# Moving the weight tiles and the shared tiles of a two-block transformer kernel by 64 bytes in the SBUF partition

## The chip, the cores and the metric

One core of one Trainium2 chip runs the whole kernel. The metric is the device time of one execution in microseconds; the kernel before has a median of 3667.25 us over three runs (3667.17 to 3675.36).

## The reference

Two transformer blocks follow each other over a sequence of 512 tokens of 1024 channels, two layers each, in float32. The first block has adaptive modulation, a SwiGLU feed-forward (FFN) before and after a mixer of sparse attention and a gated MLP. The second has pooling in its first layer and attention over latent and context tokens in its second, each followed by a squared-ReLU MLP; the 256 context tokens go through the first layer only. Nearly all of the arithmetic is dense matrix products such as

```python
def _swiglu(x, w_in, w_out):
    a, b = jnp.split(x @ w_in, 2, axis=-1)
    return (jax.nn.silu(a) * b) @ w_out
...
def sq_relu_mlp(h, w_in, w_out):
    return jnp.square(jax.nn.relu(h @ w_in)) @ w_out
```

## The kernel before

Activations are held with channels on the partitions, in 8 chunks of 128, and 512 tokens along the partition. A product is made in three TensorE passes: each operand x is split into a high part (x rounded to `float32r`) and a low part (x minus the high part), and `mm3` (lines 113 to 116) adds high x high, high x low and low x high in one PSUM bank. `dense` (line 118) does that over the 8 chunks of the contraction, 24 matmuls of 128 x 128 weights and 512 (or, for context tokens, 256) columns.

`T.matmul(ps, w, x)` takes the weights as the stationary operand and the activations as the moving one. In the products that leave tokens on the partitions (`tok_proj`, lines 619 and 1431, and `values`) the activations are the stationary operand and 256 or 280 columns of weights move.

The weights come by DMA on SP's queue, 4 KB of each partition at a time, into `raw` (`wload`, line 91). `wsplit` (line 96) makes `whi` on ScalarE and `wlo` on VectorE, or on GpSimd where `cur["lo"]` says so. `raw`, `whi` and `wlo` have three buffers each, so a product's weights are made while the one before it runs. Products whose weights go at once are `Pre.issue` (line 283, matmuls on line 301) and `Pre.product` (line 328); they start on `h` times its gains before the norm is known.

The moving operands are these tiles:

- `n0` and `n1` (in the trace `n`), the normed input of a block, and `m` in the mixer's output product, 8 chunks each;
- `r`, 16 tiles of 512 columns (line 111) that hold hidden units, heads, or what `Pre` uses;
- `hid`, a few more tiles for hidden units. `HID_R` (line 468) says which of a part's 8 chunks lie in `hid` (0) and which in `r` (1). The FFN's hidden units go in parts of 8, 8 and 6 chunks; the last part lies in `hid` alone, but for the last FFN. The MLPs of the second block have two of eight chunks in `hid`, with `q` 0 and 4 (lines 1365 and 1583);
- `nc` and `hc`, for the context tokens: 256 columns, moved against the same `whi` and `wlo`. Their products are woven between those of the latent tokens (`weave`, line 1318).

The pools are laid out in the partition in the order in which they are opened, each tile rounded up to 32 bytes. `top` opens `const`, `resid`, `wraw`, `whi`, `wlo`, `r`, `norm`, `shp` and `small` first (lines 60 to 68); all pools of the stages come behind `small`. `const` starts at byte 16512, a multiple of 128, and has `par` (392 columns, 1568 bytes), `ident` (512) and `ones` (8, rounded to 32): 2112 bytes, 64 more than a multiple of 128. The pools from `resid` to `shp` take multiples of 128, so they all start at 64 past a multiple, and so does `small`, whose first tile is `pad` (line 71), 32 bytes that nothing reads. `small` ends so that the pools of the stages start at a multiple of 128. Before the change the tiles lie so:

| tiles | start, beyond a multiple of 128 bytes |
|---|---|
| `h`, `raw`, `whi`, `wlo`, `r`, `norm`, `shp` | 64 |
| `n`, `m`, `nc`, `hc`; `qT`, `kT`, `vl`, `pth`, `ptl` of the attentions | 0 |
| `hid` | 0; 64 in the last FFN |
| `adaw`, `junk`, `crow` of the modulation vectors | 0; 64 in the last FFN |
| temporaries of the FFN and MLP stages (2112 bytes each) | 0 and 64 by turns |
| `ident` | 32 |

Inside a tile every chunk of weights (512 bytes) and of activations (2048 or 1024 bytes) keeps the tile's place. Nothing in the kernel orders the work by place; the order of instructions is the order of the program on each engine, apart from the weaving of fillers (`run_steps`).

Of the kernel before, what the change touches and what calls it, by code (L numbers as in the profile page):

```python
# [9 lines left out]
F32 = mybir.dt.float32  # L10
# [29 lines left out]
PCOLS = {}  # L40
_n = 0
for _name, _w in (
    ("c", 8), ("c_2", 8), ("c_ctx_2", 8), ("norm_g", 48), ("final_g", 8), ("ada_b", 144),
    ("b_ada_2", 96), ("g_mix_pre_2", 16), ("g_mix_post_2", 16), ("g_mlp_pre_2", 16),
    ("g_mlp_post_2", 16), ("pool_scale_2", 8),
):
    PCOLS[_name] = _n
    _n += _w
# [3 lines left out]
def build(tc, d, stop=99):  # L52
    nc = tc.nc
    V, A, G, T, SY = nc.vector, nc.scalar, nc.gpsimd, nc.tensor, nc.sync
    top = ExitStack()

    def pool(st, name, bufs=1, **kw):
        return st.enter_context(tc.tile_pool(name=name, bufs=bufs, reuse_waits="tile", **kw))

    const = pool(top, "const")  # L60
# [7 lines left out]
    small = pool(top, "small", 2)  # L68
    aux = pool(top, "aux", 2, space=PSUM)

    G.memset(small.tile([128, 8], F32, name="pad", tag="pad", bufs=1), 0.0)

    par = const.tile([128, NPC], F32, name="par")
    SY.dma_start(par, d["par"])
    ident = const.tile([128, 128], F32, name="ident")
    ones = const.tile([128, 2], F32, name="ones")
    V.memset(ones, 1.0)
    h = resid.tile([128, DC, S], F32, name="h")

# [1640 lines left out]
```

## Time and profile before

| | |
|---|---|
| median of three runs | 3667.25 us (3667.17 to 3675.36) |
| the profiled execution's own time | 3675.36 us |
| its span, first to last instruction | 3673.6 us |
| instructions | 44524, of them 16932 matmuls |
| mean granted TensorE clock | 0.973 |
| DMA | 455.24 MB, 124 GB/s over the span |

PE stands for TensorE's matmuls, PEld for its weight loads, DVE for VectorE, ACT for ScalarE, POOL for GpSimd and SP for the engine whose queue issues the DMAs. A row `mm<-n,whi` is a matmul that writes the tile `mm` and reads `n` and `whi`; L114 is line 114. Matmuls overlap, so a row's mean duration is longer than the time from one matmul's start to the next one's. A clock of 1.00 is 2.4 GHz, 0.50 is 1.2 GHz.

### The profile page before, as it was taken

The page shows a single profiled execution, that of the slowest core. Times are in us where ns is not written, and L with a number is a line of the kernel's source. Part 1 is how long each engine was busy: PE and PEld are TensorE (multiplying, and loading weights), DVE is VectorE, ACT ScalarE, POOL GpSimd, SP SyncE. Part 2 cuts the span into 40 slices and gives each one's busy share as a digit, 9 for nine tenths or more (in the row PEclk, how much of TensorE's full clock was granted, in tenths as well). Part 3 has the DMA queues.
Part 4 walks back from the last instruction along what each step waited for, and adds up shares of the span by engine and source line. Part 5 has one row for each costly group of instructions (what it writes and reads, how often), then busy time and mean ns, then how long its engine had stood idle before and what let it go on. Part 6 is the DMA issues. An engine that isn't in the chain of part 4 may idle for free.

```text
span 3673.6 us, 44524 instructions
## 1 busy us (share of the span) xinstructions
PE 3491.0 (95%) x16932; PEld 2880.7 (78%) x16932; DVE 2301.8 (63%) x3656; ACT 1450.0 (39%) x2467; POOL 522.1 (14%) x493
## 2 busy tenths in 40 slices
PE   6999999999999999999999999989999978989998
PEld 5888886788878888887787877778888878767886
DVE  8863777458754995488647855665444587655434
ACT  4222465433223322366634223544333344634222
POOL 3000413030001200142004000340000052130000
PEclk8999989999999999999999999979999988999999
DMA  6862321237852573221134842314334331013332
GB/s 239 283 207 92 99 71 47 71 116 246 293 182 92 179 240 126 92 94 58 44 100 160 284 139 85 95 40 128 119 119 122 113 113 59 7 41 101 95 98 69
DMA packets 139254, 455.24 MB, mean 124 GB/s; under 512 B 16676, under 2 KB 19104, under 8 KB 138912
## 3 DMA queue, kind: packets, MB, share of 16 engines
q1 hardware_dynamic: 139040, 452.39, 38.1%
q8 instruction: 133, 2.18, 0.2%
q14 instruction: 81, 0.66, 0.1%
HBM read 450.23 MB, written 2.10 MB: 123 GB/s over the span
## 4 chain that ended last, share of the span: by engine, by line
PE 45%; DVE 6%; POOL 2%; ACT 2%; issue 1%; DMA 1%; DVEq 0%; SPq 0%; ACTq 0%; POOLq 0%
PE mm L114 12%; PE mm L116 12%; PE mm L115 12%; DVE ssum L150 1%; POOL shp L269 1%; DVE h L1077 1%; PE aux L862 0%; PE aux L1540 0%; PE mm L1443 0%; PE mm L1444 0%; PE mm L1445 0%; PE o L830 0%; POOL shp L274 0%; DVE wlo L100 0%; ACT whi L98 0%
## 5 line engine op out<-in xcount | busy, mean ns | idle before, releaser
L98 ACT ACTIVATE whi<-raw 128x1024 fp32r<-128x1024 f32 (+2 forms) x636 | 620.1, 977 | 1504.8 <-PE mm L115 1018.9
L100 DVE TENSOR_TENSOR wlo<-raw,whi 128x1024 fp32r<-128x1024 f32 (+3 forms) x584 | 677.9, 1162 | 513.1 <-ACT whi L98 507.9
L114 PE MATMUL mm<-n,whi 128*128 128x512 f32 x2096 | 831.8, 397 | 13.8 <-ACT nt L220 9.2
L116 PE MATMUL mm<-n,wlo 128*128 128x512 f32 x2096 | 826.0, 395 | 7.1 <-DVE wlo L100 7.0
L115 PE MATMUL mm<-n,whi 128*128 128x512 f32 x2096 | 823.5, 393 | 0.4 <-DVE n L224 0.2
L116 PEld LDWEIGHTS mm<-n,wlo 128*128 128x128 f32 x2096 | 396.0, 189 | 98.7 <-DVE wlo L100 10.4
L114 PEld LDWEIGHTS mm<-n,whi 128*128 128x128 f32 x2096 | 396.7, 189 | 97.7 <-issue 11.3
L115 PEld LDWEIGHTS mm<-n,whi 128*128 128x128 f32 x2096 | 396.4, 189 | 85.6 <-DVE n L224 0.9
L399 DVE SCALAR_TENSOR_TENSOR junk<-adaw,crow 128x1024 f32<-128x1024 f32 x288 | 353.4, 1227 | 78.9 <-DMA adaw<-adaT 58.8
L114 PE MATMUL mm<-r,whi 128*128 128x512 f32 x960 | 380.5, 396 | 6.5 <-ACT whi L98 5.9
L116 PE MATMUL mm<-r,wlo 128*128 128x512 f32 x960 | 379.1, 395 | 0.0
L115 PE MATMUL mm<-r,whi 128*128 128x512 f32 x960 | 376.1, 392 | 0.8 <-DVE r L108 0.8
L150 POOL TENSOR_TENSOR ssum<-ssum,sq 128x512 f32<-128x512 f32 x30 | 45.4, 1514 | 1293.7 <-ACT sq L149 1293.6
L114 PEld LDWEIGHTS mm<-r,whi 128*128 128x128 f32 x960 | 181.1, 189 | 45.8 <-ACT whi L98 6.4
L116 PEld LDWEIGHTS mm<-r,wlo 128*128 128x128 f32 x960 | 180.9, 188 | 42.2 <-DVE wlo L100 0.5
L115 PEld LDWEIGHTS mm<-r,whi 128*128 128x128 f32 x960 | 181.2, 189 | 41.7 <-DVE r L108 1.4
L100 POOL TENSOR_TENSOR wlo<-raw,whi 128x1024 fp32r<-128x1024 f32 (+1 forms) x52 | 108.9, 2102 | 637.1 <-ACT whi L98 630.4
L114 PE MATMUL mm<-hid,whi 128*128 128x512 f32 x448 | 176.8, 395 | 0.0
L116 PE MATMUL mm<-hid,wlo 128*128 128x512 f32 x448 | 175.6, 392 | 0.0
L115 PE MATMUL mm<-hid,whi 128*128 128x512 f32 x448 | 174.8, 390 | 0.0
L539 DVE SCALAR_TENSOR_TENSOR h<-mm,hg,h 128x512 f32<-128x512 f32 x96 | 71.8, 748 | 134.1 <-PE mm L116 134.1
L301 PE MATMUL mm<-r,whi 128*128 128x512 f32 x384 | 128.6, 410 | 18.4 <-ACT r L241 17.0
(472 smaller groups left out, 5807.0 us busy)
## 6 DMA issues: line engine op xcount, KB each, us to landing
adaw<-adaT SPq DMA_DIRECT2D x240, 512.0 KB, 4.9
raw<-ffn_in SPq DMA_DIRECT2D x170, 512.0 KB, 4.5
raw<-mlp_in SPq DMA_DIRECT2D x96, 512.0 KB, 3.8
raw<-ffn_out SPq DMA_DIRECT2D x64, 512.0 KB, 4.1
raw<-mlp_out SPq DMA_DIRECT2D x64, 512.0 KB, 3.7
raw<-mlp_out SPq DMA_DIRECT2D x64, 256.0 KB, 2.9
raw<-ffn_out SPq DMA_DIRECT2D x32, 384.0 KB, 3.1
raw<-mix_zb SPq DMA_DIRECT2D x16, 512.0 KB, 3.5
```

Source lines behind the costliest of these rows:

```text
L98: A.activation(hi[:, :F], raw, AF.Copy)
L100: (eng or cur["lo"]).tensor_tensor(lo[:, :F], raw, hi[:, :F], op=OP.subtract)
L114: T.matmul(ps, lh, rh, start=start, stop=False)
L115: T.matmul(ps, lh, rl, start=False, stop=False)
L116: T.matmul(ps, ll, rh, start=False, stop=stop)
L150: self.last = (eng or V).tensor_tensor(self.acc, self.acc, sq, op=OP.add)
L269: G.tensor_tensor(o.rearrange("p (k m) -> p k m", k=n), raw[:, k * 128:(k + n) * 128].rearrange("p (k m) -> p k m", k=n), self.sh[:, k:k + ...
L301: T.matmul(self.pss[n], w[:, sl], x, start=k + e == 0, stop=k == DC - 1 and e == 2)
L399: V.scalar_tensor_tensor(junk, w, 1.0, cs[v], op0=OP.mult, op1=OP.mult, accum_out=mods[v][:, j * 8 + m:j * 8 + m + 1])
L539: V.scalar_tensor_tensor(h[:, m], ps, hg[:, m:m + 1], h[:, m], op0=OP.mult, op1=OP.add)
L1077: V.tensor_tensor(x[:, k], t, x[:, k], op=OP.add)
```

## The change

`par` loses three groups of columns, 24 in all (96 bytes), that no line reads: `c`, `c_2` and `c_ctx_2` come by DMAs of their own (line 388). `const` gets a tile `pad0` of 32 bytes behind `ones`. Together `const` becomes 2048 bytes, and the pools from `resid` to `shp` start 64 bytes lower, at multiples of 128. `pad` in `small` grows by 64 bytes, so that everything behind it keeps its address. `ident` moves from 32 to 64 past a multiple of 128. No product, split or copy is changed, nor is the order of anything; one memset of GpSimd is added. In the table above the first row becomes 0, `ident` 64, and the rest stays.

```diff
 for _name, _w in (
-    ("c", 8), ("c_2", 8), ("c_ctx_2", 8), ("norm_g", 48), ("final_g", 8), ("ada_b", 144),
+    ("norm_g", 48), ("final_g", 8), ("ada_b", 144),
     ("b_ada_2", 96), ("g_mix_pre_2", 16), ("g_mix_post_2", 16), ("g_mlp_pre_2", 16),
     ("g_mlp_post_2", 16), ("pool_scale_2", 8),
 ):
...
-    G.memset(small.tile([128, 8], F32, name="pad", tag="pad", bufs=1), 0.0)
+    G.memset(small.tile([128, 24], F32, name="pad", tag="pad", bufs=1), 0.0)
 
     par = const.tile([128, NPC], F32, name="par")
     SY.dma_start(par, d["par"])
     ident = const.tile([128, 128], F32, name="ident")
     ones = const.tile([128, 2], F32, name="ones")
+
+    G.memset(const.tile([128, 8], F32, name="pad0"), 0.0)
     V.memset(ones, 1.0)
     h = resid.tile([128, DC, S], F32, name="h")
```

## Rows read from the trace of the kernel before

**Rows 1.** Busy times of the page: us, share of the span, instructions.
```profile
PE 3491.0 (95%) x16932; PEld 2880.7 (78%) x16932; DVE 2301.8 (63%) x3656; ACT 1450.0 (39%) x2467; POOL 522.1 (14%) x493
```

**Rows 2.** Busy time by stage: us, busy of each engine, PEclk, DMA share, GB/s.
```profile
92.00:410.00 318.00, 315.86 (x1373) 257.52 (x1371) 190.33 (x261) 93.43 (x116) 17.53 (x17) 0.99 0.54 181
776.50:819.00 42.50, 42.50 (x187) 34.75 (x186) 29.79 (x33) 18.68 (x26) 23.08 (x22) 1.00 0.34 107
1330.00:1418.00 88.00, 88.00 (x386) 72.19 (x385) 76.86 (x120) 25.26 (x32) 0.00 (x0) 1.00 0.65 209
3231.00:3273.00 42.00, 42.00 (x187) 34.75 (x186) 14.87 (x14) 16.40 (x26) 20.73 (x26) 1.00 0.26 80
```

**Rows 3.** Groups by line and form: count, busy us, mean ns, idle before.
```profile
L114 PE MATMUL mm<-n,whi 128*128 128x512 f32 x2096 | 831.8, 397 | 13.8 <-ACT nt L220 9.2 <-DVE rp L645 4.2 <-DVE px L377 0.3
...
L114 PE MATMUL mm<-r,whi 128*128 128x512 f32 x960 | 380.5, 396 | 6.5 <-ACT whi L98 5.9 <-ACT r L107 0.5
...
L114 PE MATMUL mm<-hid,whi 128*128 128x512 f32 x448 | 176.8, 395 | 0.0
...
L114 PE MATMUL mm<-nc,whi 128*128 128x256 f32 x272 | 79.5, 293 | 9.4 <-ACT nc L107 9.1 <-ACT whi L98 0.2
```

**Rows 4.** One tile's matmuls (n, m) in two stretches: ns min/median/max, first and last start.
```profile
L116 PE MATMUL mm<-n,wlo x128: 392/392/394, 1330.5 to 1417.7; 128*128 128x512 f32 x128
...
L116 PE MATMUL mm<-m,wlo x64: 387/394/397, 776.2 to 819.5; 128*128 128x512 f32 x64
```

**Rows 5.** The same view of r, attention's output product, 3229 to 3276 us.
```profile
L115 PE MATMUL mm<-r,whi x64: 389/389/393, 3230.6 to 3273.4; 128*128 128x512 f32 x64
L116 PE MATMUL mm<-r,wlo x64: 388/389/389, 3230.8 to 3273.7; 128*128 128x512 f32 x64
```

**Rows 6.** Timeline of PE in an FFN output product: start, duration.
```profile
161.14 0.40 PE L114 MATMUL mm<-hid,whi 128*128 128x512 f32 x1
...
162.53 0.40 PE L114 MATMUL mm<-r,whi 128*128 128x512 f32 x1
...
164.62 0.39 PE L114 MATMUL mm<-r,whi 128*128 128x512 f32 x1
...
166.66 0.40 PE L114 MATMUL mm<-hid,whi 128*128 128x512 f32 x1
```

**Rows 7.** Timeline of PE, matmuls of 256 columns in two stages.
```profile
2804.91 0.28 PE L114 MATMUL mm<-hc,whi 128*128 128x256 f32 x1
...
2805.97 0.39 PE L114 MATMUL mm<-hid,whi 128*128 128x512 f32 x1
...
3099.74 0.28 PE L1443 MATMUL mm<-whi,r 128*128 128x256 f32 x1
...
3100.82 0.28 PE L1443 MATMUL mm<-whi,r 128*128 128x256 f32 x1
```

**Rows 8.** Line 399 on VectorE, from 1330 to 1418 and from 2100 to 2188 us.
```profile
L399 DVE SCALAR_TENSOR_TENSOR junk<-adaw,crow x41: 1215/1224/1227, 1329.2 to 1401.3; 128x1024 f32<-128x1024 f32 x41
...
L399 DVE SCALAR_TENSOR_TENSOR junk<-adaw,crow x14: 1216/1226/1227, 2099.1 to 2131.0; 128x1024 f32<-128x1024 f32 x14
```

**Rows 9.** DMA issues (KB each, median us to landing), and the memset of pad.
```profile
raw<-ffn_in SPq DMA_DIRECT2D x12, 256.0 KB, 6.0
h<-xT SPq DMA_DIRECT2D x8, 256.0 KB, 6.3
...
L71 POOL MEMSET pad<- x1: 105/105/105, 0.7 to 0.7; 128x8 f32 x1
```

**Rows 10.** Timeline of PE, two runs in the second attention.
```profile
3140.79 0.39 PE L114 MATMUL o<-pth,vl 128*128 128x512 f32 x1
...
3141.47 0.60 PE L1540 MATMUL aux<-ident,p 128*128 128x128 f32 x4
...
3168.01 0.40 PE L114 MATMUL o<-pth,vl 128*128 128x512 f32 x1
...
3170.10 0.27 PE L202 MATMUL aux<-ident,rs 128*128 128x128 f32 x1
```

## The prediction

> **What bounds the kernel now.** I read the busy times first: PE is busy for 95% of the span [rows 1]. The table by stage says it more sharply: from 92 to 410 us PE is busy for 315.86 of 318.00 us, VectorE for 190.33 and ScalarE for 93.43 [rows 2]. PE sets the pace of this kernel, and what makes its matmuls longer or shorter is mostly on the path. So the question is a small one, asked many times: how far apart do two dense matmuls start? The groups by form give the counts [rows 3]: with 512 columns, three lines times 2096 on `n`, 960 on `r`, 448 on `hid`; with 256 columns, three times 272 on `nc`. By the loops of the context's second product there are three times 256 on `hc`.
>
> The reader should not look at the mean duration of a matmul (395 ns and the like): they overlap. The pitch is what counts, the time from one start to the next, and two streams of like products differ in it, though the granted clock is 1.00 in each, 2.4 GHz, and PE never rests [rows 2]. In a product on `n`, line 116 starts 128 times from 1330.5 to 1417.7 us: 87.2 us for 127 triples, 381 matmuls, 228.9 ns each; in the mixer's output product on `m`, 43.3 us for 189, 229.1 ns [rows 4]. In the attention's output product on `r`, line 115 gives 42.8 us for 189, 226.5 ns, and line 116 42.9, 227.0 ns: 226.7 between them [rows 5]. The weights are in the same `whi` and `wlo` in all of them, at 64 past a multiple of 128 bytes. The moving operand is not: `n` and `m` lie at a multiple of 128, `r` at 64 past one. Where both operands of a matmul stand equally to 128 bytes, it takes about 2.3 ns less than where they stand 64 apart (229.0 is the mean of the first two).
>
> The timeline of an FFN output product shows the same law from a second side [rows 6]. Its 24 matmuls have two `hid` tiles (at 0) and then six `r` (at 64). From 161.14 to 162.53 us are the six matmuls on `hid`: 231.7 ns. The first nine on `r` go to 164.62 us: 232.2 ns. The last nine go to 166.66 us: 226.7 ns. So an equal pair doesn't settle at once; it needs some ten matmuls, and here it is thrown out again every 24. Over the period the pitch is 5.52 us / 24 = 230.0 ns.
>
> **The change part by part.** `const` and `small` trade 64 bytes, and `h`, `raw`, `whi`, `wlo`, `r`, `norm` and `shp` between them move from 64 to 0; all else stays. Each pair of weights and `n`, `m`, `hid` or `r` becomes an equal one, at 0, with one exception: `hid` in the last FFN stays at 64.
>
> *Pure streams.* `n` has 3 x 2096 = 6288 matmuls; `m` 64 x 3 in each of two layers, 384 [rows 4]; the last, six-tile part of three FFN blocks 144 on `hid` alone, 432. That is 7104 matmuls, at 229.0 - 226.7 = 2.3 ns: **16.3 us off**.
>
> *Mixed streams.* `r` has 2880 less the 192 that are already equal [rows 5], `hid` 1344 less 432: 3600. In the last FFN all 528 (parts of 8, 8 and 6 chunks, each for 8 outputs in three passes) are equal pairs now, which leaves 3072. At 230.0 - 226.7 they would give 3.3 ns each; in other stages the operands change sides less often, so I take 3.0: **9.2 us off**. The last FFN's first two parts, 384 matmuls, get the mixture instead, 3.3 ns more: **1.3 us back**. Line 301's on `r` are equal now and stay so: nothing.
>
> *Restarts.* Each stream that starts anew after a wait, a transpose or a product of another width will be unsettled for its first ten matmuls, some 5 ns each (the 232.2 above against 226.7); the unequal streams of now lose less there. Context products alone break in 816/24 + 768/12 = 98 times [rows 3]; with waits, means and transposes I estimate 250 breaks. Streams on `r` pay this today, and a stream cut short pays in part; so I take 20 ns of the 50: **5.0 us back**. Bounds: 0 and 12.5.
>
> *256 columns go the other way.* Nine matmuls on `hc` (0) against `wlo` and `whi` (64) take 2804.91 to 2805.97 us, 117.8 ns; nine in the query product, with `r` and `whi` both at 64, take 3099.74 to 3100.82 us, 120.0 ns [rows 7]. The 1584 on `nc` and `hc` become equal pairs, at 2.2 ns more: **3.5 us back**. Bounds: 0 and 3.5.
>
> *Other engines.* Line 399 on VectorE reads and writes tiles at 0 in the first of two windows and at 64 in the second: 1224 and 1226 ns [rows 8]. So ScalarE's and VectorE's splits of `raw` stay as they are: 0. DMAs into `h` (64) land in 6.3 us, those of the same size into the first block's weights in `hid` (0) in 6.0 [rows 9]; eight loads of `h` at 0.3 us overlap others, so between 0 and 2.4 us in the opening; I take 0. `ident` moves from 32 to 64, still unequal to what it transposes; of its some 600 transposes no row is at 64, so I bound them by the 2.2 ns that placing makes in rows 7, plus or minus 1.3 us, and take 0. `par` loses 24 columns that nothing reads. The new memset is one more like the 105 ns of `pad` [rows 9] on POOL in the first microsecond, under the first loads; uncovered it would cost those 0.1 us. No instruction else is added, and no wait.
>
> The sum is 16.3 + 9.2 - 1.3 - 5.0 - 3.5 = 15.7 us. The profiled execution took 3675.4 us, 8 more than the median of 3667.25; the sum is taken from both alike: 3660 for a run like the profiled one, and **3651.6 us** for the median, 0.43% less. What would be late next is the supply of weights by ScalarE and VectorE; a product of 24 takes 5.44 us then instead of 5.49, and with VectorE busy for at most 76.86 of 88.00 us in these stretches [rows 2] it doesn't close in.
>
> **A rule against it.** The rows 4 to 6 say that moving and stationary reads disturb each other. The Trainium skill, "TensorE: Matmul & The Clock Gate", section "Step-by-step: what each phase is for", says that the array has two independent read ports, one for the streamed operand and one for the weights; and "SBUF — State Buffer", "Specifications (TRN2)", gives lines of 16 bytes, which a move by 64 doesn't cut differently. By these the placing could not matter, and the sum would be 0. The trace disagrees: 226.7 against 229.0 ns over hundreds of matmuls.
>
> **The rivals.** *Nothing that can be measured:* the pitch of rows 5 comes from something else in that stage, say its DMA share of 0.26 against 0.34 and 0.65 [rows 2], or the gain is eaten by restarts at their upper bound and by stages where PE waits for the splits of attention. For: the transposes and softmax stages do hold PE up. Against: rows 6, where pitch settles and unsettles within 5 us under the same traffic. Prices: 3667 with no effect, 3659 at half of it. Chances: 0.08 for no effect, 0.12 for half, and 0.02 for pools that the allocator rounds otherwise than I added them up, which gives 3667 too. The two read ports of the Trainium skill's page on TensorE, named above, would make it the 3667.
>
> *Slower:* the pair at 0 and 0 never settles. No stream of such pairs in this trace is longer than nine: those from 3168.01 to 3170.10 us take 232.2 ns each [rows 10]. If all remained like that, the pure streams would lose 7104 x 3.2 ns, the mixed ones 3072 x 2.2 and the last FFN 384 x 5.5, 31.6 us, and with the 3.5 of the narrow ones the time is 3702. It decides at the tenth matmul of a stream. Against it: three at the end of another such run, 3140.79 to 3141.47 us, have the settled 226.7 [rows 10]. Chance: 0.06.
>
> **How the numbers follow.** About 0.3%, 11 us, is what can be told from no change here. The forecast, pairs at 0 settle like pairs at 64, has 0.72. Within it the gain goes from 24.2 us (restarts and narrow products cost nothing) to 6.9 (restarts at their bound, and the transposes too), the time from 3643 to 3660; 0.03 of the 0.72 lie within 11 us. So faster 0.69, same 0.25 (the 0.03 and the 0.22 of the first rival), slower 0.06. The range takes in the lower end with the 2.4 us of the opening's DMAs and 2 us of scatter, and reaches up over no change: 3639 to 3668.
>
> **What would show it.** In the profile after: products on `n` and `m` at 226.7 ns, long runs without the 229 and 232 of now; the FFN output products at 226.7 throughout their 24; `hc` at 120.0; mean durations on VectorE and ScalarE unchanged; all of the gain in PE's busy time. I am wrong if products on `n` stay at 228.9, or show 232, or if their pitch falls and the span doesn't.

## The result, and the profile after

The changed kernel is slower. Its median is 3694.83 us (five runs, 3689.89 to 3705.65), that of the kernel before in the same five rounds 3673.55 us (3667.17 to 3675.83); the ratio is 1.0066, with a 95% interval of 1.0052 to 1.008. The forecast was 3651.6 us, with 3639 to 3668 as its range. The profiled execution after took 3693.08 us (span 3691.3, mean granted clock 0.974, where before had 0.973). Lines behind `ones` stand two further on in the changed file: `mm3` is L116 to L118, the splits are L100 and L102. The runs below differ in how many lines they add, so the same line has other numbers there.

The page's busy times, the answer to [rows 1]:

```profile
PE 3513.6 (95%) x16932; PEld 2877.9 (78%) x16932; DVE 2303.9 (62%) x3656; ACT 1452.0 (39%) x2467; POOL 521.9 (14%) x494
```

TensorE is busy for 22.6 us more; VectorE and ScalarE moved by 2 us, GpSimd by 0.2. The same work takes TensorE longer. The busy times of four stretches like those of [rows 2] (us, busy of PE, PEld, DVE, ACT and POOL, PEclk, DMA share, GB/s) say that it isn't a wait either:

```profile
92.00:410.00 318.00, 315.35 (x1358) 254.82 (x1357) 187.17 (x259) 91.78 (x115) 14.43 (x14) 0.99 0.53 180
775.00:820.00 45.00, 45.00 (x195) 36.37 (x194) 30.68 (x36) 19.88 (x29) 24.04 (x24) 1.00 0.32 105
1331.00:1421.00 90.00, 90.00 (x387) 72.41 (x387) 77.74 (x120) 25.28 (x32) 0.00 (x0) 1.00 0.63 206
3247.00:3289.00 42.00, 42.00 (x187) 34.80 (x186) 14.71 (x14) 16.18 (x25) 21.12 (x27) 1.00 0.27 85
```

TensorE is as full as it was, at 0.99 to 1.00 of its clock, and from 92 to 410 us it starts 1358 matmuls where it started 1373. So the pitch again. One tile's matmuls (`n`, `m`, `r`) in the stretches of [rows 4, 5]; columns as there:

```profile
L118 PE MATMUL mm<-n,wlo x128: 392/395/398, 1331.7 to 1420.6; 128*128 128x512 f32 x128
...
L118 PE MATMUL mm<-m,wlo x64: 387/393/404, 775.4 to 819.4; 128*128 128x512 f32 x64
...
L117 PE MATMUL mm<-r,whi x64: 389/389/395, 3246.2 to 3289.0; 128*128 128x512 f32 x64
L118 PE MATMUL mm<-r,wlo x64: 388/389/393, 3246.4 to 3289.3; 128*128 128x512 f32 x64
```

On `n` it is 88.9 us / 381 = 233.3 ns, where [rows 4] gave 228.9; on `m` 44.0 / 189 = 232.8 instead of 229.1. On `r`, 42.8 and 42.9 / 189 = 226.5 and 227.0, it is what it was. The pairs that were meant to come down to the pitch of `r` went up by 4 ns. The timeline of an FFN output product (start, duration), beside [rows 6]:

```profile
160.57 0.40 PE L116 MATMUL mm<-hid,whi 128*128 128x512 f32 x1
...
161.96 0.39 PE L116 MATMUL mm<-r,whi 128*128 128x512 f32 x1
...
166.06 0.40 PE L116 MATMUL mm<-hid,whi 128*128 128x512 f32 x1
```

Six on `hid` have 231.7 ns as before; the 18 on `r` take 4.10 us, 227.8 ns each; the period is 5.49 us instead of 5.52. And the timeline of twelve matmuls of 256 columns on `hc`, for [rows 7]:

```profile
2806.07 0.28 PE L116 MATMUL mm<-hc,whi 128*128 128x256 f32 x1
...
2807.51 0.39 PE L116 MATMUL mm<-hid,whi 128*128 128x512 f32 x1
```

That is 1.44 us / 12 = 120.0 ns, from 117.8.

**The account.** One stretch is not the whole trace: after the change, of 148 products of 24 on `n` that run without a break, 102 have 233.3 ns and nearly all others 232.1 to 233.1. So the table below takes, over each whole trace, the mean step from one start to the next, of the 512-column matmuls of `mm3` the steps between 215 and 260 ns, of the narrow ones those between 100 and 140. The others, in which TensorE waits or runs at its lower clock, are left out.

| matmuls | count | before, ns | after, ns | together, us |
|---|---|---|---|---|
| on `n` | 6288 | 229.1 | 233.0 | +24.4 |
| on `m` | 384 | 229.2 | 232.8 | +1.4 |
| on `hid` alone | 432 | 228.9 | 233.3 | +1.9 |
| mixed products, on `r` | 2688 | 230.0 | 228.9 | -3.0 |
| mixed products, on `hid` | 912 | 230.2 | 232.3 | +1.9 |
| on `nc` and `hc` | 1584 | 117.9 | 119.1 | +1.8 |

That is 28.4 us. The two profiled spans differ by 17.7 us and the medians by 21.3, so the steps account for all of the loss, and some of that is given back elsewhere: all steps over 260 ns together, where TensorE waits or its clock is lower, take 5 us less than before.

### The profile page after: what moved, and what is told of

Same layout as the page of the kernel before. It is cut to its first block, busy times and chain, and to the rows that moved or that the text cites. A ratio compares the mean times of both kernels' runs of the same rounds, so it can differ in the third digit from the quotient of the medians.

```text
span 3691.3 us, 44525 instructions
## 1 busy us (share of the span) xinstructions
PE 3513.6 (95%) x16932; PEld 2877.9 (78%) x16932; DVE 2303.9 (62%) x3656; ACT 1452.0 (39%) x2467; POOL 521.9 (14%) x494
## 4 chain that ended last, share of the span: by engine, by line
PE 47%; DVE 6%; ACT 2%; issue 1%; POOL 1%; DMA 0%; DVEq 0%; ACTq 0%; POOLq 0%
PE mm L116 13%; PE mm L118 13%; PE mm L117 13%; PE mm L303 1%; DVE ssum L152 1%; DVE h L1079 1%; PE aux L864 0%; PE aux L1542 0%; PE o L832 0%; PE mm L1445 0%; PE mm L1446 0%; PE mm L1447 0%; ACT whi L100 0%; PE o L833 0%; PE o L117 0%
## 5 line engine op out<-in xcount | busy, mean ns | idle before, releaser
L100 ACT ACTIVATE whi<-raw 128x1024 fp32r<-128x1024 f32 (+2 forms) x636 | 620.8, 978 | 1527.5 <-PE mm L117 1041.2
L102 DVE TENSOR_TENSOR wlo<-raw,whi 128x1024 fp32r<-128x1024 f32 (+3 forms) x584 | 678.9, 1163 | 525.5 <-ACT whi L100 519.4
L116 PE MATMUL mm<-n,whi 128*128 128x512 f32 x2096 | 834.8, 398 | 13.7 <-ACT nt L222 9.2
L118 PE MATMUL mm<-n,wlo 128*128 128x512 f32 x2096 | 832.5, 398 | 4.4 <-DVE wlo L102 4.3
L117 PE MATMUL mm<-n,whi 128*128 128x512 f32 x2096 | 833.4, 398 | 0.4 <-DVE n L226 0.2
L116 PEld LDWEIGHTS mm<-n,whi 128*128 128x128 f32 x2096 | 396.8, 189 | 108.5 <-issue 11.3
L118 PEld LDWEIGHTS mm<-n,wlo 128*128 128x128 f32 x2096 | 396.2, 189 | 99.4 <-DVE wlo L102 7.4
L117 PEld LDWEIGHTS mm<-n,whi 128*128 128x128 f32 x2096 | 396.6, 189 | 92.9 <-POOL n L110 1.2
L116 PE MATMUL mm<-r,whi 128*128 128x512 f32 x960 | 377.9, 394 | 7.4 <-ACT whi L100 5.8
L117 PE MATMUL mm<-r,whi 128*128 128x512 f32 x960 | 377.4, 393 | 0.2 <-DVE r L110 0.2
L118 PE MATMUL mm<-r,wlo 128*128 128x512 f32 x960 | 376.8, 392 | 0.0
L116 PEld LDWEIGHTS mm<-r,whi 128*128 128x128 f32 x960 | 181.0, 189 | 48.3 <-ACT whi L100 6.2
L117 PEld LDWEIGHTS mm<-r,whi 128*128 128x128 f32 x960 | 181.1, 189 | 40.2 <-DVE r L110 0.5
L118 PEld LDWEIGHTS mm<-r,wlo 128*128 128x128 f32 x960 | 180.9, 188 | 39.9 <-issue 0.5
L102 POOL TENSOR_TENSOR wlo<-raw,whi 128x1024 fp32r<-128x1024 f32 (+1 forms) x52 | 109.9, 2122 | 638.8 <-ACT whi L100 636.7
L118 PE MATMUL mm<-hid,wlo 128*128 128x512 f32 x448 | 177.1, 395 | 0.0
L116 PE MATMUL mm<-hid,whi 128*128 128x512 f32 x448 | 176.9, 395 | 0.0
L117 PE MATMUL mm<-hid,whi 128*128 128x512 f32 x448 | 175.9, 393 | 0.0
```

Of the source, the lines that this page charges most:

```text
L100: A.activation(hi[:, :F], raw, AF.Copy)
L102: (eng or cur["lo"]).tensor_tensor(lo[:, :F], raw, hi[:, :F], op=OP.subtract)
L116: T.matmul(ps, lh, rh, start=start, stop=False)
L117: T.matmul(ps, lh, rl, start=False, stop=False)
L118: T.matmul(ps, ll, rh, start=False, stop=stop)
```

## The experiments

**Theory.** What counts is not how the two operands of a matmul stand to 128 bytes but how they stand to each other over 256: the address of the moving operand less that of the weights, modulo 256. Below this is called the difference. Added up over the pools, the weights and `r` start 192 past a multiple of 256 bytes in the kernel before, and 128 past one in the changed one; `n`, `m`, `nc`, `hc` and nearly all `hid` start at a multiple of 256 in both. So the difference of the products on `n` was 64 and is now 128, and that of `r` is 0 in both. **Rivals:** the place modulo 128 counts, as forecast, and something else in the change (an edit, the new place of `h` or `raw`) costs the time; or pairs at multiples of 128 never settle, whatever their difference (the forecast's slower rival). Ratios below are to the kernel before, run beside each kernel on the same chip.

**1. The weights 64 bytes up instead of down.** `mc1` moves from `small` to `const`, which grows by 64 bytes; all that the change moved goes to a multiple of 256, and the difference is 0 nearly everywhere (not for `hid` in the last FFN). The diff is to the kernel before.

```diff
-    ml1, mc1 = mods_tile("ml1", 48), mods_tile("mc1", 16)
+    ml1, mc1 = mods_tile("ml1", 48), const.tile([128, 16], F32, name="mc1", tag="mc1")
```

> Weights and shared tiles 64 bytes higher than before instead of 64 lower: weights, n, m, hid, nc, hc and r then all lie at multiples of 256 bytes. Theory A: the pitch goes by (moving operand minus weights) modulo 256: 0 gives 226.7 ns, 64 gives 229.0, 128 gives 232.4 to 233.3. It expects 226.7 on n, m and hid, 16 us less than before, ratio 0.9957 (0.992 to 0.998). Theory B: what counts is each operand's own place against 128 bytes, and both at a multiple of 128 is bad for n, m and hid. It expects 232 to 233 on them as in the kernel after, ratio 1.006.

Measured: 3659.15 us (ten runs, 3653.9 to 3666.96) against 3672.79; ratio 0.9962, 0.995 to 0.9973. This kernel beats both. The matmuls on `n` in the stretch of [rows 4], and in one in the second block:

```profile
L116 PE MATMUL mm<-n,wlo x128: 389/389/389, 1320.8 to 1407.2; 128*128 128x512 f32 x128
...
L116 PE MATMUL mm<-n,wlo x128: 389/389/389, 2095.0 to 2181.4; 128*128 128x512 f32 x128
```

Both are 86.4 / 381 = 226.8 ns, and not one duration differs from the next. In the first stretch `n` and the weights are equal modulo 512 bytes too, in the second they are 256 apart: the period is 256. The FFN output product on its timeline:

```profile
160.01 0.39 PE L114 MATMUL mm<-hid,whi 128*128 128x512 f32 x1
...
165.45 0.39 PE L114 MATMUL mm<-hid,whi 128*128 128x512 f32 x1
```

5.44 us / 24 = 226.7 ns, throughout, as the forecast had said of equal pairs. So pairs at multiples of 128 do settle, and the rival of pairs that never settle falls.

**2. The weights 128 below the kernel before.** They come to 64 past a multiple of 256, and the difference on `n` to 192. The diff is to the changed kernel.

```diff
-    G.memset(small.tile([128, 24], F32, name="pad", tag="pad", bufs=1), 0.0)
+    G.memset(small.tile([128, 32], F32, name="pad", tag="pad", bufs=1), 0.0)
...
-    ones = const.tile([128, 2], F32, name="ones")
+    ones = small.tile([128, 2], F32, name="ones", tag="ones", bufs=1)
...
-    G.memset(const.tile([128, 8], F32, name="pad0"), 0.0)
```

> Weights and shared tiles 128 bytes lower than before: n, m, hid lie 192 beyond the weights modulo 256 (before: 64, after: 128). Theory A has no row for 192; if the law is even about 0 it expects 229.0 ns on n as before and a ratio of 1.000 (0.998 to 1.003), if 192 is worse than 128, up to 236 ns and 1.010; r stays equal to the weights and settles at 226.7. Theory B (place against 128 bytes alone) expects exactly the kernel before: 229.0, ratio 1.000.

Measured: 3691.52 us (3686.91 to 3696.8); ratio 1.005, 1.0033 to 1.0068. The two tiles' matmuls, `n` and then `r`:

```profile
L116 PE MATMUL mm<-n,whi x128: 394/394/394, 1336.1 to 1425.0; 128*128 128x512 f32 x128
...
L116 PE MATMUL mm<-r,whi x64: 389/389/395, 3249.6 to 3292.5; 128*128 128x512 f32 x64
```

`n` takes 88.9 / 381 = 233.3 ns. To 128 bytes everything stands as in the kernel before, which has 228.9, so the rule over 128 bytes falls. But 64 and 192 are not alike, as one branch of the expectation had it, and 192 is no worse than 128, as the other had it: it costs the same. `r` stays at 42.9 / 189 = 227.0.

**3. All edits of the change, no move.** `pad0` takes 64 bytes more and `pad` 64 less, so that `resid` to `shp` stay where they were before. The diff is to the changed kernel.

```diff
-    G.memset(small.tile([128, 24], F32, name="pad", tag="pad", bufs=1), 0.0)
+    G.memset(small.tile([128, 8], F32, name="pad", tag="pad", bufs=1), 0.0)
...
-    G.memset(const.tile([128, 8], F32, name="pad0"), 0.0)
+    G.memset(const.tile([128, 24], F32, name="pad0"), 0.0)
```

> All edits of the change, with pad0 64 bytes larger and pad 64 smaller, so that no weights and no shared tiles move; only par's columns, ident (to 64) and ones move. Theories A and B: n at 229.0 ns, ratio 1.000 (0.998 to 1.002). Theory C, the loss comes from ident, par or the extra memset: ratio 1.006, pitches on n as before.

Measured: 3674.37 us; ratio 1.0006, 0.9996 to 1.0016. The shorter `par`, the moved `ident` and the added memset cost nothing that can be told. `n` keeps its 87.2 / 381 = 228.9 ns:

```profile
L118 PE MATMUL mm<-n,wlo x128: 392/392/394, 1320.6 to 1407.8; 128*128 128x512 f32 x128
```

**4. Only `h` and `raw` moved.** The kernel before with the change's `const`, and a pool of 64 bytes ahead of `whi`. The diff is to the changed kernel.

```diff
+    gap = pool(top, "gap")
+    G.memset(gap.tile([128, 16], F32, name="gap"), 0.0)
     whi_p = pool(top, "whi", 3)
...
-    G.memset(small.tile([128, 24], F32, name="pad", tag="pad", bufs=1), 0.0)
+    G.memset(small.tile([128, 8], F32, name="pad", tag="pad", bufs=1), 0.0)
```

> Of the move only h and raw: 64 bytes lower as in the kernel after, with 64 unused bytes behind raw, so that whi, wlo, r, norm and shp stay as before. Theories A and B: n at 229.0 ns, ratio 1.000 (0.998 to 1.002). Theory D, the splits or the DMAs into raw slow down or are held up at the new place: part or all of the ratio 1.006, with longer rows on the lines of whi and wlo.

Measured: 3674.57 us; ratio 1.0004, 0.9993 to 1.0016. The groups of the splits (busy us, mean ns of one, idle before) have the 977 and 1160 ns of one that they have elsewhere (978 and 1163 in the changed kernel):

```profile
L102 ACT ACTIVATE whi<-raw 128x1024 fp32r<-128x1024 f32 (+2 forms) x636 | 620.3, 977 | 1501.4 <-PE mm L119 1027.6
L104 DVE TENSOR_TENSOR wlo<-raw,whi 128x1024 fp32r<-128x1024 f32 (+3 forms) x584 | 677.1, 1160 | 511.4 <-ACT whi L102 505.6
```

What is left of the change is the move of `whi`, `wlo`, `r`, `norm` and `shp`.

**5. The changed kernel, with the stages' tiles moved after it.** The weights stay at 128; `n`, `m`, `nc`, `hc` and `hid` go up by 128 (the small tile `mv` changes its pool to make room). The difference is 0 again, but neither operand lies at a multiple of 256.

```diff
-    G.memset(small.tile([128, 24], F32, name="pad", tag="pad", bufs=1), 0.0)
+    G.memset(small.tile([128, 48], F32, name="pad", tag="pad", bufs=1), 0.0)
...
-        mv = gm.tile([128, 4, 2], F32, name="mv")
+        mv = small.tile([128, 4, 2], F32, name="mv", tag="mv", bufs=1)
```

> Weights and r stay where the change put them, at 128 past a multiple of 256 bytes; n, m, nc, hc and hid move up by 128, to 128 past one as well, so that the difference between moving operand and weights is 0 modulo 256. Theory A (the pitch goes by the difference between moving and weight address modulo 256): the products on n and m have 226.7 ns where the changed kernel has 233.3, and the time is that of the kernel with all at a multiple of 256, a ratio of 0.996 to the kernel before. Rival (what counts is that each operand lies at a multiple of 256 bytes by itself): no pair lies at one, n and m stay at 232 to 233 ns or get worse, ratio 1.006 or more. Rival (pages of 512 bytes count): no size of its own; a pitch between those two.

Measured: 3655.47 us (eight runs, 3645.95 to 3670.19); ratio 0.9953, 0.9938 to 0.9968.

```profile
L116 PE MATMUL mm<-n,whi x128: 389/389/389, 1323.9 to 1410.3; 128*128 128x512 f32 x128
```

86.4 / 381 = 226.8 ns. It is the difference that counts, not the place of either operand. With the weights where the change put them, the kernel gains 0.5% instead of losing 0.7%. Run 1 has the weights and `n` at 0, this run has them at 128.

**6. The changed kernel, with `r`, `norm` and `shp` 128 up.** Now `r` stands 128 from the weights, like `n`.

```diff
+    gap = pool(top, "gap", 2)
     r_p = pool(top, "r", 16)
...
-            mx = small.tile([128, 16], F32, name="mxc", tag="mxc")
+            mx = gap.tile([128, 16], F32, name="mxc", tag="mxc")
```

> The changed kernel with only r, norm and shp moved up by 128 bytes: r then lies at a multiple of 256, 128 away from the weights, like n. Theory A: the attention's output product on r, which has 226.7 ns in every kernel so far, goes to 232 to 233 ns, 192 matmuls by 6 ns, 1 us; the other 3400 on r lose between 0 and 6 ns each, so the time goes up from the changed kernel by 1 to 20 us, ratio 1.007 to 1.012 to the kernel before. Rival (tiles r are read faster for another reason, such as the stage they are in): 226.7 ns stay, ratio 1.0066.

Measured: 3697.98 us (3696.24 to 3699.3); ratio 1.0066, 1.005 to 1.0083. The output product on `r`, which had 226.5 to 227.0 ns in every kernel above:

```profile
L119 PE MATMUL mm<-r,wlo x64: 392/398/398, 3250.6 to 3294.7; 128*128 128x512 f32 x64
```

44.1 / 189 = 233.3 ns. So nothing in that tile or stage is special. The whole moves less than that suggests. The FFN output product's timeline has a period of 5.58 us, 0.09 more than in the changed kernel:

```profile
160.34 0.39 PE L117 MATMUL mm<-hid,whi 128*128 128x512 f32 x1
...
165.92 0.39 PE L117 MATMUL mm<-hid,whi 128*128 128x512 f32 x1
```

By that row the 3600 mixed matmuls, 150 times 24, would lose 13.5 us against the changed kernel; over the whole trace their steps, taken as in the account above, lose 10.2. TensorE is busy for 6.8 us more:

```profile
PE 3520.4 (95%) x16932; PEld 2874.4 (78%) x16932; DVE 2301.7 (62%) x3656; ACT 1449.6 (39%) x2467; POOL 521.6 (14%) x494
```

The medians differ by 3 us, and the ratios, with 5 to 6 us of uncertainty each, can't be told apart. The mean granted clock works the other way, 0.973 to 0.976 in this run's executions and 0.970 to 0.974 in the changed kernel's; how much that hides was not tested. The pitch of `r` is settled by this run; what the whole kernel pays for it is not.

**7. All equal but `wlo`.** Run 1's kernel, with `wlo` behind `shp` and 128 bytes further on: one matmul in three has a difference of 128. The diff is to run 1.

```diff
-    wlo_p = pool(top, "wlo", 3)
...
     shp_p = pool(top, "shp")
+    gap = pool(top, "gap", 2)
+    wlo_p = pool(top, "wlo", 3)
...
-            mx = small.tile([128, 16], F32, name="mxc", tag="mxc")
+            mx = gap.tile([128, 16], F32, name="mxc", tag="mxc")
```

> All pairs at a multiple of 256 bytes as in the run with mc1 moved, but the tiles wlo 128 further on, so that one matmul in three has weights 128 away from its moving operand. Theory A with the matmul's own weights: two pitches of 226.7 and one of 233.3 in each three, mean 228.9 ns on n, the long one the step that starts with the matmul on wlo; with the weights that are loaded beside it (those of the matmul that follows): the same mean, the long one the step that starts with the matmul before, that on whi with the low part. Time between the two kernels, ratio 0.998 to 1.002. Rival (any switch between weights at different places unsettles the whole stream): 232 ns or more on all three, ratio 1.004 or more.

Measured: 3689.43 us (3688.61 to 3696.14); ratio 1.0049, 1.0034 to 1.0064. Neither form of theory A gave this time; the rival's did, but it had all three steps long.

```profile
L115 PE MATMUL mm<-n,whi x128: 389/389/389, 1328.7 to 1416.8; 128*128 128x512 f32 x128
L116 PE MATMUL mm<-n,whi x128: 396/396/397, 1328.9 to 1417.0; 128*128 128x512 f32 x128
L117 PE MATMUL mm<-n,wlo x128: 397/397/397, 1329.2 to 1417.2; 128*128 128x512 f32 x128
```

88.1 / 381 = 231.2 ns, two thirds of the way from run 1's 226.8 to the changed kernel's 233.3, for one odd matmul in three. In the trace's records the starts lie on the mean 226.7 ns apart from L115 to L116, 232.5 from L116 to L117, and 234.2 from L117 to the next L115. Two steps are long: that of the matmul whose own weights are at the odd difference, and that of the one before it, beside which those weights are loaded. I had put the price on one of them. The price doesn't add up over the two: in the changed kernel a matmul's own weights and those loaded beside it are both at 128, and its mean step is 233.3. Since the first step stays at 226.7, the rival of a stream that is unsettled as a whole falls.

**8. The narrow products at a difference of 192.** In run 2 the matmuls on `nc` and `hc`, at a difference of 192, had a mean step of 115.7 ns, the lowest of any run (means of 256-column steps are taken as in the account above). Here run 1's kernel gets that difference for `nc` and `hc` alone; the diff is to run 1. **Run 9** is run 1's kernel again, on the same chip.

```diff
+    G.memset(pool(nst, "gap", 1).tile([128, 48], F32, name="gap"), 0.0)
     nc_p = pool(nst, "ncp", 8)
+    G.memset(pool(nst, "gap2", 1).tile([128, 16], F32, name="gap2"), 0.0)
...
+        G.memset(pool(st, "gap3", 1).tile([128, 48], F32, name="gap3"), 0.0)
         hc_p = pool(st, "hidc", 4)
```

> The kernel with mc1 moved (all pairs equal modulo 256 bytes), and the moving operands of the context's products, nc and hc, 192 bytes further on, where the run with the weights 128 lower had the lowest pitch of 256-column matmuls, 115.65 ns. Theory: products of 256 columns want the moving operand 192 past the weights, where those of 512 want it at the same place, so nc and hc go from 119.5 to about 115.7 ns; 1584 matmuls by 3.8 ns are 6.0 us, a ratio to the kernel before 0.0016 below that of the kernel with mc1 moved. Rival: the 115.65 ns came from the weights' or the operand's own place or from what stands around those products, and nc and hc stay at 117.5 to 119.5 ns: no change that can be told.

> The kernel with mc1 moved once more, as the base that the kernel with nc and hc 192 further on is compared with on the same chip: 512-column products at 226.7 ns, 256-column ones at 119.5, ratio 0.995 to 0.997 to the kernel before.

Measured: 3658.16 us, ratio 0.9953 (0.9936 to 0.997), against 3659.17 us and 0.9963 (0.9949 to 0.9977). They can't be told apart. Twelve matmuls on `hc` on the timeline, first of run 9, then of run 8:

```profile
2802.98 0.28 PE L114 MATMUL mm<-hc,whi 128*128 128x256 f32 x1
...
2804.30 0.28 PE L116 MATMUL mm<-hc,wlo 128*128 128x256 f32 x1
```

```profile
2803.07 0.28 PE L114 MATMUL mm<-hc,whi 128*128 128x256 f32 x1
...
2804.37 0.28 PE L116 MATMUL mm<-hc,wlo 128*128 128x256 f32 x1
```

1.32 and 1.30 us over eleven steps, 120.0 and 118.2 ns; over the whole trace the mean on `nc` and `hc` falls from 119.5 to 117.2, not to the 115.7 of run 2 at the same difference. Nor do the kernel before, 117.9, and run 3, 117.3, agree quite, though no operand of these products differs in place. So for 256 columns the difference is not all that counts, and what else does stays open. The price of a wrong guess here is small: 1584 x 2.3 ns are 3.6 us.

## Why the prediction was wrong

**The step that failed** is the premise of the sum: "Where both operands of a matmul stand equally to 128 bytes, it takes about 2.3 ns less than where they stand 64 apart." The rows it came from had two kinds of pair, `r` with the weights and `n` with the weights. The first are equal to 128 bytes, and also to 256; the second 64 apart, by 128 as by 256. The rows could not tell the two laws apart, and I took the one in which the change was worded. The second witness, [rows 6], has the same two kinds. The third, the settled run of [rows 10], is on `vl` and `pth`, which are equal to 256 bytes as well; it spoke against the rival of pairs that never settle, and not for 128. So "each pair of weights and `n`, `m`, `hid` or `r` becomes an equal one, at 0" was true of 128 bytes and false of what counts: on `n` the difference went from 64 to 128.

**Pure streams**, 16.3 us off: all 7104 went to a difference of 128 and lose 27.7 us by the account above. Run 1, in which the pairs are equal in fact, has 226.8 ns where the sum had 226.7. **Mixed streams**, 9.2 us off, 1.3 back: 1.1 us off here, because `r` gains and `hid` loses; in run 1 the FFN product has the 226.7 throughout. **Restarts**, 5.0 us back, were only argued, and no run takes them by themselves; in run 1's trace the 512-column steps exceed 226.7 ns by 5 us in all, which is the size that was put in. **256 columns**, 3.5 us back: 120.0 ns came in the stretch shown, as said, though from another cause, as the difference was 128; over the trace it is 1.8 us.

The sum of 15.7 us, 0.43%, is close to what the runs with equal pairs gave (0.38% in run 1, 0.47% in run 5, both intervals hold it). In part that is luck. By the account's steps run 1 saves 24.0 us on 512 columns, where the forecast had 19.2 after restarts, and gives 2.6 back on 256; of these 21.4 us the medians show 13.6. What took the rest was not tested. The granted clock is a candidate: it averages 0.972 over run 1's ten executions and 0.974 over those of the kernel before beside them, and within run 1 the execution at 0.970 takes 3666.76 us, those at 0.974 take 3655.12 and 3655.90.

**Other engines**, 0: right, by runs 3 and 4 and by line 399 (401 now) on VectorE, whose median is 1224 ns, as in [rows 8]:

```profile
L401 DVE SCALAR_TENSOR_TENSOR junk<-adaw,crow x41: 1218/1224/1227, 1330.6 to 1403.8; 128x1024 f32<-128x1024 f32 x41
```

**The rivals.** The slower one, "the pair at 0 and 0 never settles", gave 3702 us, 7 from the median, by pitches of 232.2 where 233 came. It was right in what is to be seen and wrong in why: pairs at multiples of 128 settle in run 1 (at 0) and run 5 (at 128), and in the changed kernel itself on `r`. It had a chance of 0.06 because only one explanation of the two pitches had been considered. "Nothing that can be measured" is refuted by the pitch of `n`, and with it the reason given for it: the pitch of `r` does not come from the traffic of its stage, since run 6 takes it away in the same stage. The two independent read ports of the Trainium skill, "TensorE: Matmul & The Clock Gate", section "Step-by-step: what each phase is for", would have made all these layouts alike. The runs disagree: the changed kernel and run 1 have the same products, with the weights 128 bytes apart, and ratios of 1.0066 and 0.9962.

## What to carry to other kernels

Where dense 512-column matmuls bound a kernel, add up the addresses of the moving tiles and of the weights in the partition and make their difference a multiple of 256 bytes; here, against a difference of 64, that is worth 0.4 to 0.5%, and a difference of 128 or 192 costs 0.5 to 0.7%. These are products in `float32r` in which each matmul loads its own 128 x 128 weights; no others were tried. When rows of two kinds suggest a law, ask which other law the same rows allow (128 or 256 bytes, absolute or relative) before the sum is built on one of them; where the rows can't decide, the other law is a rival with a real chance. One layout each for 0, 64, 128 and 192 is a cheap search.

## What the runs showed of the hardware

The pitch of 512-column matmuls on `n`, at a granted clock of 1.00, by the difference of moving operand and weights modulo 256 bytes:

| difference | pitch, ns | kernel |
|---|---|---|
| 0 | 226.8 | runs 1 and 5 |
| 64 | 228.9 | before, run 3 |
| 128 | 232.1 to 233.3 | changed, run 6 |
| 192 | 233.3 | run 2 |

It is not symmetric, and only multiples of 64 bytes were tried. In the stretch shown of the changed kernel, at 128, the steps are not even: they alternate between 229 or 230 and 237 or 238 ns, while in run 2, at 192, each is 233 or 234. A step is long when the matmul's own weights are at 128, and also when only the weights loaded beside it are (run 7); whether one of these is an after-effect of the other was not told apart. Why two streams that only read should disturb each other so was not shown by any run. For 256 columns the order is another, and the runs scatter: 119.6 ns at 0 (run 1), 119.1 at 128 (changed), 117.9 or 117.3 at 64 (before, run 3), 115.7 or 117.2 at 192 (runs 2 and 8).
